# Five blocks of up columns per MLP instead of four: 2048 plain, then four times 512 plain and 1024 by Strassen's product

## The chip, the cores and the metric

The kernel runs on one core of a Trainium2 chip. The metric is the device time of one execution in microseconds; the median of three runs is given. The engines are called as in the profile: PE is TensorE, DVE is VectorE, ACT is ScalarE, POOL is GpSimd, and SP's queue issues most of the DMAs.

## The reference

A two-layer decoder trunk over 256 tokens of width 2048, all in float32. Layer 0 mixes by a state-space scan and by stick-breaking attention, layer 1 by a pooling mixer; each mixer is followed by the same MLP, and the MLPs are what the change is about. Cut to what matters:

```python
def sq_relu_mlp(h, w_up, w_down):        # h: (256, 2048)
    u = jax.nn.relu(h @ w_up)            # w_up: (2048, 8192)
    return (u * u) @ w_down              # w_down: (8192, 2048)

for layer in range(2):
    x = x + mixer(rms_norm(x, ...), ...)
    x = x + sq_relu_mlp(rms_norm(x, mlp_norm[layer]), mlp_w_up[layer], mlp_w_down[layer])
```

## The kernel before

**Precision.** Every float32 operand is split into two parts, `hi` (rounded to the type TensorE multiplies fast, by ACT, L235) and `lo` (what is left, by DVE, L236). A product is done as hi x hi + lo x hi + hi x lo, so each tile of weights costs three matmuls of a token half (128 tokens) by 512 columns.

**The stream of weights.** `plan()` writes down, by hand and before anything is issued, the order of all work as a list of units and of steps. A unit is a block of output columns, a step one load of up to 512 KB: two tiles of 128 x 512 or four of 128 x 256. `feed(i)` runs ahead of the products: SP's queue loads the raw weights of a step nine steps ahead into seven buffers (`raw`, L206), and `split(i)` splits them three steps ahead into four buffers each of `hi` and `lo`. A scheduler then orders the instructions of each engine by this order and by what is ready; each engine works through its own row in order.

**The MLP.** The 8192 hidden columns are done in four blocks of 2048. A block has two parts.

- Up: plain units of 256 columns (kind `up`). Their result stands with the hidden columns on the partitions, as the down product wants it. For each of the 16 tiles of a unit TensorE does two pairs of a 512-wide matmul (L963) and a 256-wide one (L965), 32 pairs a unit. At the end of a unit `finish` adds the halves (ACT L324, DVE L325), applies relu and the norm's row (DVE L874) and leaves the rest to `gen_u`: the square (ACT L681), its `hi` (ACT L279) and its `lo` (DVE L280). Two units fill one u tile of four rows.
- Down: four units of 512 output columns (kind `down`), each over the block's 16 rows of tiles of u, two rows and 12 matmuls (L971) a step, eight steps a unit. Each unit's result is added into `x_sb` by DVE (L834), one addition per token half.

The first block's up columns are all plain: eight units. In the other three blocks 1024 of the 2048 columns are plain, four units, and 1024 are done by Strassen's product of 2 x 2 blocks with seven products instead of eight (kinds `sa` and `sb`, matmuls L734). Both are issued during the down product of the block before: `sa` in 12 steps, `sb` in eight pairs of steps, whose weights DVE combines first by four subtractions a pair (L222 to L225). A step has two products of three 512-wide matmuls. `due(i)` says after how many of the 32 down steps the i-th piece comes. `gen_s` then puts the products together on DVE and ACT and turns the result by 16 transposes on TensorE (L294) during the next block's up units. It runs in `lane`, a queue of work that advances by one stage a step.

**The end of layer 0.** After the first column group of the last down product, `finish` loads what the pooling mixer wants into the buffers that u held: the bias into u's rows 0 to 3 and the scale into rows 4 to 7 (L850), the pooling matrix into rows 8 to 11 (L843). Each load waits until the last column group has read those rows. DVE multiplies bias and scale (L854) and adds them to `x_sb` (L765), ACT converts the matrix (L845). The normed `x_sb` is turned by transposes (L294), multiplied by `pool_w` (L971), its result scaled and split (ACT L863, DVE L864), and the pooling matrix applied (L776 to L780).

The lines that set the order:

```python
            for i in range(8 if b == 0 else 4):
                unit("w_up", D * layer, KT, b * FB + 256 * i, 256, "up", (layer, b, i), ...
            if b + 1 < NB:
                for kind in ("sa", "sb"): ...
    def due(i):
        return 1 + 10 * i // 12 if i < 12 else 13 + 19 * (i - 12) // 8
```

## Time and profile before

| what | value |
| --- | --- |
| three runs | 2163.53, 2164.75, 2165.72 us; median 2164.75 |
| the profiled execution, its own time | 2164.82 us |
| its span, first to last instruction | 2163.0 us |
| granted TensorE clock, mean | 1.000 |
| HBM read | 450.32 MB, mean of all DMA 210 GB/s |
| DMA engines busy in a block's down part (1170.4 to 1296.1 us) | 0.76, 251 GB/s |
| DMA engines busy in a block's plain up part (1124.2 to 1170.4 us) | 0.58, 182 GB/s |
| DVE busy in these two | 100.8 of 125.7 us; 29.1 of 46.2 us |
| ACT busy in these two | 69.6 of 125.7 us; 24.8 of 46.2 us |

Matmuls overlap in the profile: a busy time for a group of them counts the overlap twice, so the pace is read from start to start, or from the pieces of the chain of waits. An idle time before an instruction is given in brackets with what ended it. The rows that carry the argument stand in the prediction.

### The profile page before, as it was taken

What the parts mean: (1) busy time and instruction counts of PE and PEld (TensorE: products, weight loads), DVE (VectorE), ACT (ScalarE), POOL (GpSimd) and SP (SyncE); (2) the same over time, 40 slices, a digit from 0 to 9 for tenths busy, and PEclk for the clock granted to TensorE, in tenths of its full rate; (3) what the DMA queues carried; (4) which work ended last, traced back from release to release, by engine and by line L of the source; (5) the groups of instructions that cost most, each with busy time, mean ns of one, the idle gap of its engine ahead of it and who ended that gap; (6) DMA issues with size and microseconds to landing.
All of it is one profiled execution on the core that took longest, in us unless ns stands there. A gap on an engine that the chain in (4) does not pass through costs nothing.

```text
span 2163.0 us, 28389 instructions
## 1 busy us (share of the span) xinstructions
PE 2154.4 (100%) x10613; PEld 1820.6 (84%) x10613; DVE 1541.7 (71%) x1908; ACT 1203.2 (56%) x1401; POOL 21.7 (1%) x21
## 2 busy tenths in 40 slices
PE   9999999999999999999999999999999999999999
PEld 8888888888888888888888888878888888888888
DVE  6988766656545586876886886578778678678754
ACT  7665456665644465555555555456555555555543
POOL 0000000000000000000000000000000000000000
PEclk9999999999999999999999999999999999999999
DMA  9665455555665567777776776565677677677663
GB/s 334 204 204 166 159 184 166 175 166 166 207 192 191 170 197 240 245 232 215 248 247 202 246 253 186 187 224 162 197 257 250 194 245 243 214 247 238 224 204 117
DMA packets 129002, 454.32 MB, mean 210 GB/s; under 512 B 14496, under 2 KB 17248, under 8 KB 128608
## 3 DMA queue, kind: packets, MB, share of 16 engines
q1 hardware_dynamic: 128000, 451.36, 64.4%
q8 instruction: 83, 1.36, 0.3%
q10 hardware_dynamic: 864, 1.15, 0.2%
q14 instruction: 55, 0.45, 0.1%
HBM read 450.32 MB, written 2.13 MB: 209 GB/s over the span
## 4 chain that ended last, share of the span: by engine, by line
PE 97%; DVE 1%; DMA 1%; issue 0%; ACT 0%; SPq 0%; DVEq 0%; ACTq 0%
PE acc L971 58%; PE acc L963 16%; PE bg L734 10%; PE acc L965 9%; PE bg L294 1%; PE bg L522 1%; DVE lo L236 0%; DMA raw<-w_all 0%; PE bg L579 0%; PE bg L669 0%; PE bg L614 0%; DMA st<-prow_in 0%; DVE st L765 0%; PE bg L610 0%; PE bg L671 0%
## 5 line engine op out<-in xcount | busy, mean ns | idle before, releaser
L235 ACT ACTIVATE hi<-raw 128x1024 fp32r<-128x1024 f32 (+2 forms) x846 | 887.6, 1049 | 889.8 <-PE acc L971 586.2
L236 DVE TENSOR_TENSOR lo<-raw,hi 128x1024 fp32r<-128x1024 f32 (+2 forms) x846 | 1012.2, 1206 | 454.7 <-ACT hi L235 432.4
L971 PE MATMUL acc<-hi,st 128*128 128x512 f32 (+2 forms) x3840 | 1165.6, 386 | 0.9 <-ACT hi L235 0.9
L971 PEld LDWEIGHTS acc<-hi,st 128*128 128x128 f32 x3840 | 710.9, 188 | 142.1 <-ACT hi L235 2.4
L971 PE MATMUL acc<-lo,st 128*128 128x512 f32 (+2 forms) x1920 | 736.2, 385 | 0.4 <-DVE lo L236 0.3
L963 PE MATMUL acc<-st,hi 128*128 128x512 f32 x1568 | 552.4, 394 | 0.0
L965 PE MATMUL acc<-st,lo 128*128 128x256 f32 x1568 | 441.8, 282 | 0.0
L971 PEld LDWEIGHTS acc<-lo,st 128*128 128x128 f32 x1920 | 360.6, 188 | 74.1 <-DVE lo L236 2.2
L963 PEld LDWEIGHTS acc<-st,hi 128*128 128x128 f32 x1568 | 294.3, 188 | 62.1 <-issue 1.4
L965 PEld LDWEIGHTS acc<-st,lo 128*128 128x128 f32 x1568 | 296.3, 189 | 2.0 <-issue 1.4
L734 PE MATMUL bg<-hi,st 128*128 128x512 f32 x672 | 206.9, 389 | 0.0
L734 PEld LDWEIGHTS bg<-hi,st 128*128 128x128 f32 x672 | 126.1, 188 | 26.3
L734 PE MATMUL bg<-lo,st 128*128 128x512 f32 x336 | 130.7, 389 | 0.0
L734 PEld LDWEIGHTS bg<-lo,st 128*128 128x128 f32 x336 | 63.1, 188 | 13.0
L834 DVE TENSOR_TENSOR st<-st,acc 128x512 f32<-128x512 f32 (+1 forms) x74 | 46.4, 669 | 15.9 <-PE acc L971 15.6
L222 DVE TENSOR_TENSOR raw<-raw 128x512 f32<-128x512 f32 x48 | 33.1, 689 | 31.1 <-DMA raw<-w_all 31.0
L223 DVE TENSOR_TENSOR raw<-raw,raw 128x512 f32<-128x512 f32 x48 | 33.1, 690 | 20.7 <-DMA raw<-w_all 19.9
L282 ACT ACTIVATE st<-bg,prm 128x256 fp32r<-128x256 f32 x64 | 28.4, 467 | 22.5 <-DVE st L283 20.9
L325 DVE TENSOR_TENSOR ev<-acc,ev 128x512 f32<-128x512 f32 x40 | 27.4, 686 | 11.6 <-ACT ev L324 11.6
L283 DVE SCALAR_TENSOR_TENSOR st<-bg,prm,st 128x256 fp32r<-128x256 f32 x64 | 29.5, 481 | 8.2 <-ACT st L282 8.2
L225 DVE TENSOR_TENSOR raw<-raw 128x512 f32<-128x512 f32 x48 | 33.1, 690 | 1.0
L224 DVE TENSOR_TENSOR raw<-raw,raw 128x512 f32<-128x512 f32 x48 | 32.9, 686 | 0.2
(187 smaller groups left out, 949.7 us busy)
## 6 DMA issues: line engine op xcount, KB each, us to landing
raw<-w_all SPq DMA_DIRECT2D x818, 512.0 KB, 3.8
raw<-w_all SPq DMA_DIRECT2D x20, 256.0 KB, 2.8
st<-x_in SPq DMA_DIRECT2D x8, 512.0 KB, 7.8
st<-scr SPq DMA_DIRECT2D x8, 512.0 KB, 6.1
raw<-w_all SPq DMA_DIRECT2D x8, 288.0 KB, 8.1
st<-prow_in SPq DMA_DIRECT2D x2, 1024.0 KB, 6.3
st<-xt_in SPq DMA_DIRECT2D x6, 256.0 KB, 7.4
st<-pmat_in SPq DMA_DIRECT2D x1, 768.0 KB, 6.2
```

The source lines that it names most:

```text
L222: dve.tensor_tensor(raw[:, 0], raw[:, 1], raw[:, 0], ALU.subtract)
L223: dve.tensor_tensor(raw[:, 1], two[:, 0], raw[:, 1], ALU.subtract)
L224: dve.tensor_tensor(two[:, 0], two[:, 0], raw[:, 0], ALU.subtract)
L225: dve.tensor_tensor(two[:, 1], two[:, 0], two[:, 1], ALU.subtract)
L235: act.activation(hi, raw, AF.Copy)
L236: dve.tensor_tensor(lo, raw, hi.bitcast(F32), ALU.subtract)
L283: dve.scalar_tensor_tensor(dst[:, 1, c], ps, gain, dst[:, 0, c].bitcast(F32), ALU.mult, ALU.subtract)
L734: pe.matmul(sps[q], st[h], w[:, j], start=p == 0 and w is hi and h == 0, stop=p == KT // 2 - 1 and w is lo)
L834: dve.tensor_tensor(x_sb[m][:, cs], x_sb[m][:, cs], ps[:, m, : d["n"]], ALU.add)
L963: pe.matmul(ps[:, f].rearrange("p (h t) -> p h t", h=2), hi[:, kk, fs], t[:, :, c], start=first, stop=False)
L965: pe.matmul(ps[:, f, :T], lo[:, kk, fs], t[:, 0, c], start=False, stop=last)
L971: pe.matmul(ps[:, m, :n], t[:, h % 2, c, m * P : (m + 1) * P], (hi, hi, lo)[h][:, kk], start=first and h == 0, stop=last and h == 2)
```

## The change

The MLP of each layer is done in five blocks instead of four: one of 2048 plain columns, then four of 1536, of which 512 are plain (two units) and 1024 Strassen's. Of 8192 columns, 4096 are plain and 4096 Strassen's; before, 5120 and 3072. A later block's down product has 12 rows of tiles, so six steps a column group and 24 in all, and `due` spreads the Strassen steps over these 24. Work per weight element, the buffers and the lookahead are as before.

```diff
-FB = 2048
-NB = DFF // FB
+SW = 1024
+
+BLOCKS = ((2048, 0), (512, SW), (512, SW), (512, SW), (512, SW))
+NB = len(BLOCKS)
+BASE = [sum(map(sum, BLOCKS[:b])) for b in range(NB)]
...
-            for i in range(8 if b == 0 else 4):
-                unit("w_up", D * layer, KT, b * FB + 256 * i, 256, "up", (layer, b, i),
+            for i in range(BLOCKS[b][0] // 256):
+                unit("w_up", D * layer, KT, BASE[b] + 256 * i, 256, "up", (layer, b, i),
...
-            if b + 1 < NB:
+            if b + 1 < NB and BLOCKS[b + 1][1]:
                 for kind in ("sa", "sb"):
-                    unit("w_up", D * layer, KT, (b + 1) * FB + FB // 2, 512, kind,
+                    unit("w_up", D * layer, KT, BASE[b + 1] + BLOCKS[b + 1][0], 512, kind,
...
-                    unit("w_down", DFF * layer + b * FB, KT, c0, n, "down", (layer, b, c),
+                    unit("w_down", DFF * layer + BASE[b], sum(BLOCKS[b]) // P, c0, n, "down",
+                         (layer, b, c),
...
-    def due(i):
-        return 1 + 10 * i // 12 if i < 12 else 13 + 19 * (i - 12) // 8
+    def due(i, n):
+        a = 5 * n // 16
+        return 1 + a * i // 12 if i < 12 else a + 3 + (n - a - 3) * (i - 12) // 8
...
-            yield from to_ring(lambda m: (a, e)[m][:, q], u_blk[b % 2], 8 + 4 * q,
-                               slot(base + 2 + q), None)
+            yield from to_ring(lambda m: (a, e)[m][:, q], u_blk[b % 2],
+                               BLOCKS[b][0] // P + 4 * q, slot(base + BLOCKS[b][0] // 512 + q),
+                               None)
```

In the changed kernel the lines quoted here stand five lower up to L739 (L236 is L241, L279 is L284), six lower from L765 to L874 (L834 is L840, L854 is L860), and five lower again behind them (L963 is L968, L971 is L976).

What this moves shows at three places. The first is ACT's row at the last block of layer 0, where the last up unit ends. `ev` is that unit's result, `acc` the sum it comes from, `st` the u tile. Before, the unit is the fourth, and its u goes to the second half of the second tile:

```order
L235 ACTIVATE hi_1910_11097<-raw_1888_10950 128x1024
L324 ACTIVATE ev_1908_11091<-acc_68_11004 128x512
L235 ACTIVATE hi_1913_11116<-raw_1891_10972 128x1024
L681 ACTIVATE ev_1908_11091<-ev_1908_11091 128x512
L279 ACTIVATE st5_1901_11044<-ev_1908_11091 128x512
L235 ACTIVATE hi_1916_11137<-raw_1895_10998 128x1024
```

Now it is the second, and its u goes to the second half of the first tile:

```order
L240 ACTIVATE hi_1978_11283<-raw_1951_11110 128x1024
L329 ACTIVATE ev_1976_11277<-acc_70_11172 128x512
L240 ACTIVATE hi_1982_11309<-raw_1954_11132 128x1024
L686 ACTIVATE ev_1976_11277<-ev_1976_11277 128x512
L284 ACTIVATE st4_1980_11289<-ev_1976_11277 128x512
L240 ACTIVATE hi_1985_11327<-raw_1960_11166 128x1024
```

ACT's order is the same; the tile that L284 writes is now `st4`, which the down product reads in its second step and not, as `st5` before, in its fourth.

The second place is DVE's row in the stretch in which the `sb` steps are split, from the split that frees a buffer to the first subtraction on the weights that are loaded into it. Before, in the third block of layer 0, `raw_1714` is freed and `raw_1736` comes into its place:

```order
L236 TENSOR_TENSOR lo_1735_10064<-raw_1714_9962,hi_1734_10063 128x1024
L224 TENSOR_TENSOR raw_1726_10023<-raw_1726_10023,raw_1723_10005 128x512
L225 TENSOR_TENSOR raw_1726_10023<-raw_1726_10023 128x512
L236 TENSOR_TENSOR lo_1738_10082<-raw_1717_9974,hi_1737_10081 128x1024
L222 TENSOR_TENSOR raw_1736_10079<-raw_1736_10079 128x512
```

Now, in the second block, `raw_1464` is freed and `raw_1485` comes into its place:

```order
L241 TENSOR_TENSOR lo_1484_8592<-raw_1464_8488,hi_1483_8591 128x1024
L241 TENSOR_TENSOR lo_1487_8604<-raw_1467_8506,hi_1486_8603 128x1024
L228 TENSOR_TENSOR raw_1476_8554<-raw_1479_8573,raw_1476_8554 128x512
L229 TENSOR_TENSOR raw_1479_8573<-raw_1479_8573,raw_1476_8554 128x512
L241 TENSOR_TENSOR lo_1490_8622<-raw_1470_8518,hi_1489_8621 128x1024
L230 TENSOR_TENSOR raw_1479_8573<-raw_1479_8573 128x512
L227 TENSOR_TENSOR raw_1485_8601<-raw_1485_8601 128x512
```

Between the two stand two subtractions and a split before, three subtractions and two splits now. Over the eight pairs of a block such a distance was two subtractions and a split in half of them, or its like; now in one.

The third place is DVE's row at the end of layer 0, around the additions of the last column group (`acc_72` before, `acc_74` now) into the two halves of `x_sb` (`st12`, `st13`). Before, the bias's additions and two splits stand ahead of both:

```order
L765 TENSOR_TENSOR st12_849_4939<-st12_849_4939,st4_1936_11251 128x512
L765 TENSOR_TENSOR st13_850_4940<-st13_850_4940,st4_1936_11251 128x512
L236 TENSOR_TENSOR lo_2019_11738<-raw_1995_11602,hi_2018_11737 128x1024
L236 TENSOR_TENSOR lo_2022_11756<-raw_1999_11624,hi_2021_11755 128x1024
L834 TENSOR_TENSOR st12_849_4939<-st12_849_4939,acc_72_11608 128x512
L834 TENSOR_TENSOR st13_850_4940<-st13_850_4940,acc_72_11608 128x512
```

Now one of the two comes first, and the product with the scale and six bias additions (three such pairs) stand between them:

```order
L241 TENSOR_TENSOR lo_2067_11802<-raw_2043_11664,hi_2066_11801 128x1024
L840 TENSOR_TENSOR st12_849_4939<-st12_849_4939,acc_74_11690 128x512
L860 TENSOR_TENSOR st4_1999_11405<-st4_1999_11405,st5_2000_11406 128x512 x4
L771 TENSOR_TENSOR st12_849_4939<-st12_849_4939,st4_1999_11405 128x512
L771 TENSOR_TENSOR st13_850_4940<-st13_850_4940,st4_1999_11405 128x512
...
L840 TENSOR_TENSOR st13_850_4940<-st13_850_4940,acc_74_11690 128x512
```

The load that L860 (L854 before) waits for starts when the fourth step of the last column group is done; that group had eight steps and now has six.

More of the change, by code (lines that the diff above doesn't have):

```diff
@@ L117, in plan @@
                     at += 1
-                    while held and at >= due(20 - len(held)):
+                    while held and at >= due(20 - len(held), 2 * d["nk"]):
                         seq += held.pop(0)
@@ L945, in tile_trunk @@
                 b = d["arg"][1]
-                need(lambda: b == 0 or len(u_blk[(b - 1) % 2]) == 16)
-                for kk in range(KT):
-                    u_blk[b % 2].pop(kk, None)
+                need(lambda: b == 0 or len(u_blk[(b - 1) % 2]) == sum(BLOCKS[b - 1]) // P)
+                u_blk[b % 2].clear()
         ps = accs[u]
```

## The prediction

> **What bounds the kernel now.** I read the page's busy times and its chain of waits first.
>
> ```profile
> span 2163.0 us, 28389 instructions
> PE 2154.4 (100%) x10613; PEld 1820.6 (84%) x10613; DVE 1541.7 (71%) x1908; ACT 1203.2 (56%) x1401; POOL 21.7 (1%) x21
> ...
> PE 97%; DVE 1%; DMA 1%; issue 0%; ACT 0%; SPq 0%; DVEq 0%; ACTq 0%
> ```
>
> The chain that ended last lies 97% on TensorE, so a matmul taken away is worth its place in that chain, and a wait put before a matmul costs its full length. The profiled execution took 2164.82 us, 1.82 around a span of 2163.0; that is 0.07 from the median of 2164.75, so a sum made against 2164.82 holds for the median as well. The pieces of that chain in the third block of layer 0 give the prices:
>
> ```profile
> 1124.37 0.23 PE acc L963
> ...
> 1132.69 0.44 PE bg L294 x4
> ...
> 1170.52 2.73 PE acc L971 x12
> 1173.25 2.72 PE bg L734 x12
> 1175.97 2.72 PE acc L971 x12
> ```
>
> From 1124.37 to 1170.52 TensorE does the block's four plain up units and, between them, four groups of four transposes. 46.15 less 4 x 0.44 is 44.39 us for four units, which are 4 x 32 pairs of a 512-wide and a 256-wide matmul: 0.347 us a pair. Twelve Strassen matmuls (L734) take 2.72 us, as twelve of the down product do.
>
> **The change, by counts.** Per layer the plain up units go from 20 to 16 and one more pair of `sa` and `sb` comes. Removed: 44.39 us. Added: 56 products of three matmuls, 168 = 14 x 12, so 14 x 2.72 = 38.08 us, and the 16 transposes of one more `gen_s`, 1.76 us. That leaves 4.55 us a layer, 9.1 us for both. The down product keeps its number of matmuls; only the last column group, cut into two halves, changes:
>
> ```profile
> 2070.85 88.33 PE acc L971 x480
> ```
>
> Of these 480, three column groups are 24 steps of 2.72 us (65.3); the other 192 half-wide matmuls take 23.05, 0.120 each. Two halves cost 0.240 against 0.227 for one full matmul; the last block now has 12 rows of tiles instead of 16, so 24 such pairs become whole: 0.3 us. Counts alone: 2164.82 - 9.4 = 2155.4. Also added per layer are 12 loads of 512 KB with their splits, 32 subtractions and 8 additions into `x_sb` on VectorE. These lie beside TensorE; what they cost if that cover fails is in (c).
>
> **Waits that the change adds.** Four places, (a) to (d).
>
> (a) The first down product of the last block. The same sequence of ScalarE runs at the end of the last up unit in the kernel before, so its length can be read (a piece of the chain, then rows of the timeline: start, us, engine, line, what):
>
> ```profile
> 1342.41 2.73 PE acc L971 x12
> ...
> 1343.29 0.58 ACT L324 ACTIVATE ev<-acc 128x512 f32<-128x512 f32 x1
> 1344.94 1.07 ACT L235 ACTIVATE hi<-raw 128x1024 fp32r<-128x1024 f32 x1 [1.07 <-PE acc L971]
> 1346.01 0.63 ACT L681 ACTIVATE ev<-ev 128x512 f32<-128x512 f32 x1
> 1346.67 0.64 ACT L279 ACTIVATE st<-ev 128x512 fp32r<-128x512 f32 x1
> ...
> 1347.34 0.69 DVE L280 TENSOR_TENSOR st<-ev,st 128x512 fp32r<-128x512 f32 x1
> ```
>
> The last up matmul ends at 1342.41. The `hi` half of that unit's u is there 4.90 us later (1346.67 + 0.64), the `lo` half 5.62 us later. ScalarE stands in between for the split that waits until TensorE has left the first down step (1344.94), and the square is queued behind it. Before the change this unit is the fourth, its u is the operand of the fourth down step, three steps or 8.2 us on, and nobody waits. After it, the unit is the second, its u is the operand of the second step, 2.72 us on, and in the last block TensorE has nothing else in its row. It waits 4.90 - 2.72 = 2.2 us, does one matmul on the `hi` half (0.23) and waits 0.5 us for the `lo` half. 2.7 us a layer, 5.4 for both; between 4.4 (the `hi` half alone) and 6.4.
>
> (b) The second to fourth block have Strassen work to put there: in TensorE's order 12 matmuls of the first step and 14 of Strassen stand before the matmul in question, 26 x 0.227 = 5.9 us, and five more before the `lo` half is wanted, 7.0 us. The same chain in the third block before, with one more split in ScalarE's row:
>
> ```profile
> 1175.61 0.61 ACT L279 ACTIVATE st<-ev 128x512 fp32r<-128x512 f32 x1
> ...
> 1176.88 0.68 DVE L280 TENSOR_TENSOR st<-ev,st 128x512 fp32r<-128x512 f32 x1
> ```
>
> From 1170.52 these end after 5.7 and 7.04 us. The cover just holds: I take 0.1 us at each of six places, 0.5 in all, and 0 to 3 as bounds (half a microsecond each if one signal more lies between).
>
> (c) VectorE in the stretch where `sb` runs. Its pace there, from start to start in the timeline, and below that two rows of the table of waits (us in total, times, longest):
>
> ```profile
> 1209.60 1.22 DVE L236 TENSOR_TENSOR lo<-raw,hi 128x1024 fp32r<-128x1024 f32 x1
> ...
> 1213.91 1.07 ACT L235 ACTIVATE hi<-raw 128x1024 fp32r<-128x1024 f32 x1 [0.34 <-PE bg L734]
> ...
> 1266.31 0.69 DVE L224 TENSOR_TENSOR raw<-raw,raw 128x512 f32<-128x512 f32 x1
> 1266.92 1.22 DVE L236 TENSOR_TENSOR lo<-raw,hi 128x1024 fp32r<-128x1024 f32 x1
> 1268.05 0.68 DVE L225 TENSOR_TENSOR raw<-raw 128x512 f32<-128x512 f32 x1
> 1268.66 1.28 DVE L834 TENSOR_TENSOR st<-st,acc 128x512 f32<-128x512 f32 x2
> 1269.85 3.49 DVE L236 TENSOR_TENSOR lo<-raw,hi 128x1024 fp32r<-128x1024 f32 x3
> ...
> 1271.03 1.07 ACT L235 ACTIVATE hi<-raw 128x1024 fp32r<-128x1024 f32 x1 [1.65 <-PE acc L971]
> ...
> 1280.09 0.50 PE L971 MATMUL acc<-lo,st 128*128 128x512 f32 x1 [0.30 <-DVE lo L236]
> ...
> DVE raw L222 <- DMA raw<-w_all: 31.0, 23, 3.2
> DVE raw L223 <- DMA raw<-w_all: 19.9, 25, 2.8
> ```
>
> A split holds VectorE 1.13 us, a subtraction 0.61 to 0.72 (I take 0.64), an addition 0.60. Before, from the first subtraction of a block to its last `sb` split, VectorE has 33 splits, 32 subtractions and 5 additions, 60.8 us, and waits (31.0 + 19.9) / 6 = 8.5 us for weights: 69.3. TensorE's 17 down and 16 `sb` steps there are 17 x 2.72 + 16 x 1.36 = 68.0. So VectorE is already a little slower, and its reserve shows it. ScalarE refills a `hi` buffer when TensorE leaves it, four steps later; that start is the moment at which the step three splits earlier is taken up. The split that ends at 1210.82 is taken at 1213.91, 3.1 us in hand; the first of the three at 1269.85 ends at 1271.0 and is taken at 1271.03, nothing in hand; at 1280.09 TensorE waits 0.30 us. The stretch eats 3.1 us where the sum gives 1.3: 1.8 us are small gaps.
>
> After, the stretch has 31 splits, 32 subtractions, 7 additions: 59.7 us, for 15 down steps and 16 of `sb`, 62.6 us. That is 2.9 us in hand where there were 7.2, so all hangs on the waits for weights. A load starts when a split frees its buffer, and the waits of before fit a landing 3.6 us later (4.3 for the second buffer of a pair). Before, in half of the eight pairs only about 2.3 us of VectorE work stand between; after, in one pair, and 3.5 to 7 in the others. That gives some 3.2 us of waiting instead of 8.5: 59.7 + 3.2 + 1.8 = 64.7 against 62.6, and the loss of 2.1 is less than the 3.1 in hand. I take 1.0 us for all six new stretches; the bounds are 0 and, with the full 8.5, 6 x (59.7 + 8.5 + 1.8 - 62.6 - 3.1) = 26 us.
>
> (d) The end of layer 0. Here the chain of before already leaves TensorE (five pieces of the chain, then rows of the timeline):
>
> ```profile
> 1421.03 6.66 DMA st<-prow_in
> ...
> 1427.71 2.00 DVE st L854 x4
> ...
> 1433.83 2.27 DVE lo L236 x2
> 1436.10 0.61 DVE st L834
> ...
> 1436.75 0.44 PE bg L294 x2
> ...
> 1426.94 0.33 SPq L843 DMA_DIRECT2D st<-pmat_in  x1
> ...
> 1433.26 1.49 ACT L845 ACTIVATE st<-st 128x1536 fp32r<-128x1536 f32 x1
> ...
> 1443.06 0.75 DVE L864 SCALAR_TENSOR_TENSOR t<-acc,rstd,t 128x512 fp32r<-128x512 f32 x1
> ```
>
> The load of the scale goes into the buffer that held u's rows 4 to 7, so it starts when the fourth step of the last down group is done (1421.03) and is there 6.7 us later. Four products and six additions (L854, L765) follow to 1433.83, and behind them in VectorE's row stand two splits and the addition (L834) that the transposes at 1436.75 wait for, late by 0.32 us. The group now has six steps, not eight. From the end of its fourth step the path is 6.7 + 2.4 + 3.7 + 0.6 = 13.4 us (the two splits now stand ahead of it); TensorE has 0.44 + 2 x 2.72 to the end of the group and 2 x 2.72 + 0.3 of pool work before it wants the result: 11.6. It waits 1.8. The pooling matrix follows the sixth step, which is now the last: ScalarE converts it (L845) some 7.8 us after the group's end instead of 2.4, and the squares of the norm stand behind that. From the trace's durations in the new order (conversion, split, square and its read-out, 0.9 to the power's result as from 1439.54 to 1440.59, then on VectorE a split, four short evictions, two additions and L864), the first half of the pool's operand comes at 14.9 us after the group's end and the second, two splits later, at 17.8; TensorE arrives at 13.9 and 15.9. Two more waits of about 1.0 and 1.8. With 0.3 of before taken off: 4.3 us. Bounds 1.5 (the first wait alone) and 7 (each half as long again).
>
> **The sum:** 2164.82 - 9.4 + 5.4 + 0.5 + 1.0 + 4.3 = 2166.6 us, +0.1%.
>
> **A rule on the clock.** The longest time TensorE stood idle within the work of before is below a microsecond, and no slice shows a clock under full:
>
> ```profile
> 1467.59 0.51 PE L780 MATMUL bg<-t,st 128*128 128x512 f32 x1 [0.84 <-DVE t L864]
> ...
> PEclk9999999999999999999999999999999999999999
> ```
>
> The waits of (a) and (d) are two to three times as long. If each of the five dropped the clock to a half for one step of twelve matmuls, 2.72 us more each, the sum would be 2180. The Trainium skill, "TensorE: Matmul & The Clock Gate", section "Why this matters for your kernels", says that gaps of more than about 3 us between bursts of matmuls bring the half clock back. By that rule none of these waits, worked out as 2.7 at most, does so; no row here shows one of that length.
>
> **The rivals.**
> 1. *The cover holds everywhere.* The scheduler's order is made for such waits, and splits run 3 us ahead in most stages. Against it: in (a) nothing stands between, and in (d) the chain of before has no slack. If (a) and (d) cost half or less, 2155.4 + 2 to 5: about 2159, faster.
> 2. *VectorE becomes the bound in the Strassen stretch.* Place: the last splits of `sb` in the second to fourth block. For it: the reserve of before falls to nothing. Against it: fewer waits for weights in the new order. It decides from some 4.2 us of waiting per stretch on; each further microsecond costs TensorE six. At 6 us: 11 us in place of 1.0, 2177, slower.
> 3. *The clock drops in the new waits:* 2180.
> 4. *The change moves no work off TensorE.* By the counts above it has 168 matmuls fewer (256 - 168 - 16 = 72 a layer and 24 in the last column group); I leave this 0.02, at 2165.
>
> **How the numbers follow.** A measurement of this kernel can tell about 0.2%, 4.3 us, from no change: under 2160.4 is faster, over 2169.1 slower. The forecast, 2166.6 with a range of its own from 2161 to 2173 by the bounds of (a), (b) and (d), has 0.60: 0.47 within 0.2% and 0.13 above. Rival 1 has 0.12, rival 2 0.22, rival 3 0.04. Faster 0.12, same 0.49, slower 0.39. The range reaches from rival 1 to the middle of rival 2: 2159 to 2179.
>
> **What would show it.** In the profile after, TensorE's matmul count falls by 168 and its busy time by some 9 us; PE at the first down product of a layer's last block shows a wait on ScalarE (L284 after) of 2.2 us and on VectorE of 0.5; at the end of layer 0 its transposes wait some 1.8 us for the additions and the pool matrix product 1 and 2 us for its operand. The waits of the subtractions for weights should fall from 8.5 to about 3 us a stretch. TensorE waiting for `lo` inside the `sb` stretches, over 1 us a block, would make rival 2 right; a clock below full after a wait, rival 3; no wait at all at the two places of (a), rival 1.

## The result and the profile after

The changed kernel took 2178.72 us (median of five runs, 2176.48 to 2181.33) against 2165.72 before: a ratio of 1.0059, 95% interval 1.0048 to 1.0069. It is slower. The forecast was 2166.6 and the range 2159 to 2179, so the median lies just inside its upper end, near rivals 2 (2177) and 3 (2180); two of the five runs lie above 2179. The profiled execution took 2176.69, 11.87 more than the 2164.82 of before. From the page and the table of waits after (us in total, times, longest); the DMA row's last number is the median time from issue to landing:

```profile
span 2174.9 us, 28266 instructions
PE 2154.2 (99%) x10445; PEld 1807.9 (83%) x10445; DVE 1609.6 (74%) x2008; ACT 1226.4 (56%) x1419; POOL 21.7 (1%) x21
...
PE 90%; DVE 5%; DMA 3%; issue 2%; ACT 0%; SPq 0%; POOL 0%; DVEq 0%; ACTq 0%; POOLq 0%
...
raw<-w_all SPq DMA_DIRECT2D x844, 512.0 KB, 4.2
...
PE acc L976 <- DVE lo L241: 6.2, 6, 2.1
PE acc L976 <- ACT st L284: 4.4, 2, 2.2
PE bg L299 <- DVE st L840: 1.7, 1, 1.7
PE bg L786 <- DVE t L870: 0.9, 2, 0.7
PE bg L786 <- ACT t L869: 0.9, 2, 0.6
...
DVE raw L227 <- DMA raw<-w_all: 40.7, 32, 3.0
DVE raw L228 <- DMA raw<-w_all: 15.1, 21, 1.6
```

The matmuls went down by 168 as counted, and yet TensorE's busy time did not fall, where some 9 us less had been forecast. About 3 us of this is work at half the clock, at which a 512-wide matmul is busy 0.63 us in the profile instead of 0.39; the rest is put down to waits shorter than the modelled ends of matmuls, which no row shows one by one. Waits of TensorE that were 0.3 us for `lo` are now 6.2, and the chain that ended last lies 10% outside TensorE, mostly on VectorE and the weights' DMAs.

An idle time in brackets starts where the modelled end of the matmul before lies, so short waits hide in it. I therefore read the losses from lengths: a down part runs from the first down product of a block to the first up product of the next. In the chain of waits, for the second block of layer 0 after the change:

```profile
977.33 2.73 PE acc L976 x12
...
1081.40 0.23 PE acc L968
```

That is 104.07 us. The same two places were read for every block and every kernel below; the last part of layer 1, which no up product follows, ends with the start of its last matmul. 24 down steps and 28 Strassen steps are 456 matmuls of 0.2267 us, 103.37 us.

| kernel | six down parts with Strassen of blocks 2 to 4 | last down part, layer 0 | last down part, layer 1 | half-clock windows inside the work |
| --- | --- | --- | --- | --- |
| before (its six with Strassen: blocks 1 to 3, 32 steps each) | 751.94, by count 750.8 | 119.44 | 88.20 | 0 |
| after | 632.55 (104.07, 105.48, 104.21, 104.87, 106.12, 107.80) | 104.30 | 69.14 | 2 |
| 456 matmuls six times | 620.2 | | | |

The up parts came out as counted: 23.96 us for two units with their transposes, 46.15 before for four.

### The profile page after: what moved, and what is told of

Its sections match the earlier page's. It is cut to its first block, busy times and chain, and to the rows that moved or that the text cites. A ratio compares the mean times of both kernels' runs of the same rounds, so it can differ in the third digit from the quotient of the medians.

```text
span 2174.9 us, 28266 instructions
## 1 busy us (share of the span) xinstructions
PE 2154.2 (99%) x10445; PEld 1807.9 (83%) x10445; DVE 1609.6 (74%) x2008; ACT 1226.4 (56%) x1419; POOL 21.7 (1%) x21
## 4 chain that ended last, share of the span: by engine, by line
PE 90%; DVE 5%; DMA 3%; issue 2%; ACT 0%; SPq 0%; POOL 0%; DVEq 0%; ACTq 0%; POOLq 0%
PE acc L976 53%; PE acc L968 13%; PE bg L739 12%; PE acc L970 7%; DMA raw<-w_all 3%; DVE lo L241 3%; PE bg L299 1%; PE bg L527 1%; DVE st L840 0%; PE bg L584 0%; PE bg L674 0%; PE bg L619 0%; DVE raw L228 0%; DMA st<-scr 0%; DVE st L771 0%
## 5 line engine op out<-in xcount | busy, mean ns | idle before, releaser
L240 ACT ACTIVATE hi<-raw 128x1024 fp32r<-128x1024 f32 (+2 forms) x868 | 910.5, 1051 | 870.1 <-PE acc L976 545.2
L241 DVE TENSOR_TENSOR lo<-raw,hi 128x1024 fp32r<-128x1024 f32 (+2 forms) x868 | 1037.6, 1207 | 400.1 <-ACT hi L240 371.5
L976 PE MATMUL acc<-hi,st 128*128 128x512 f32 (+2 forms) x3824 | 1170.3, 388 | 5.4 <-ACT st L284 4.4
L976 PEld LDWEIGHTS acc<-hi,st 128*128 128x128 f32 x3824 | 710.0, 188 | 150.7 <-ACT st L284 7.0
L976 PE MATMUL acc<-lo,st 128*128 128x512 f32 (+2 forms) x1912 | 736.8, 387 | 6.4 <-DVE lo L241 6.2
L968 PE MATMUL acc<-st,hi 128*128 128x512 f32 x1312 | 464.8, 396 | 0.0
L976 PEld LDWEIGHTS acc<-lo,st 128*128 128x128 f32 x1912 | 360.0, 188 | 83.8 <-DVE lo L241 11.2
L970 PE MATMUL acc<-st,lo 128*128 128x256 f32 x1312 | 369.5, 282 | 0.0
L968 PEld LDWEIGHTS acc<-st,hi 128*128 128x128 f32 x1312 | 246.2, 188 | 51.8 <-issue 1.4
L739 PE MATMUL bg<-hi,st 128*128 128x512 f32 x896 | 277.0, 389 | 0.0
L970 PEld LDWEIGHTS acc<-st,lo 128*128 128x128 f32 x1312 | 248.0, 189 | 2.1 <-issue 1.4
L739 PEld LDWEIGHTS bg<-hi,st 128*128 128x128 f32 x896 | 168.2, 188 | 34.9
L739 PE MATMUL bg<-lo,st 128*128 128x512 f32 x448 | 174.5, 390 | 0.0
L739 PEld LDWEIGHTS bg<-lo,st 128*128 128x128 f32 x448 | 84.1, 188 | 17.8 <-DVE lo L241 0.5
L840 DVE TENSOR_TENSOR st<-st,acc 128x512 f32<-128x512 f32 (+1 forms) x90 | 57.2, 670 | 13.9 <-PE acc L976 13.6
L228 DVE TENSOR_TENSOR raw<-raw,raw 128x512 f32<-128x512 f32 x64 | 44.0, 687 | 15.3 <-DMA raw<-w_all 15.1
L229 DVE TENSOR_TENSOR raw<-raw,raw 128x512 f32<-128x512 f32 x64 | 43.9, 686 | 0.7
```

The costliest lines, as they stand in the source:

```text
L228: dve.tensor_tensor(raw[:, 1], two[:, 0], raw[:, 1], ALU.subtract)
L229: dve.tensor_tensor(two[:, 0], two[:, 0], raw[:, 0], ALU.subtract)
L240: act.activation(hi, raw, AF.Copy)
L241: dve.tensor_tensor(lo, raw, hi.bitcast(F32), ALU.subtract)
L739: pe.matmul(sps[q], st[h], w[:, j], start=p == 0 and w is hi and h == 0, stop=p == KT // 2 - 1 and w is lo)
L840: dve.tensor_tensor(x_sb[m][:, cs], x_sb[m][:, cs], ps[:, m, : d["n"]], ALU.add)
```

## The half clock

The mean granted clock of the profiled execution is 0.998, where it was 1.000 before. Windows of a quarter of a microsecond show where: at 1368.49 and at 2044.33 the granted clock falls from 1.00 to 0.50 and stays there for 3.41 us. The distance, 675.84, is 198 times 3.4133. In all later profiles the falls of one execution also lay on one grid of 3.413 us to within 0.01 us (1439.83, 2098.60 and 2166.87 in one: 193 and 20 periods). So I laid the windows on that grid. Columns: window, its length, busy time and instructions of PE, PEld, DVE, ACT, POOL, the granted clock, the DMA share, GB/s. Around the wait at the last block's first down product, in layer 0 and then in layer 1:

```profile
1365.08:1368.49 3.41, 1.13 (x4) 0.37 (x2) 3.24 (x5) 2.32 (x3) 0.00 (x0) 1.00 0.41 154
1368.49:1371.90 3.41, 3.25 (x8) 2.58 (x9) 0.10 (x1) 0.00 (x0) 0.00 (x0) 0.50 0.48 156
1371.90:1375.32 3.42, 3.42 (x17) 2.78 (x15) 1.23 (x1) 1.06 (x1) 0.00 (x0) 1.00 0.00 0
...
2102.36:2105.77 3.41, 2.44 (x11) 1.69 (x9) 2.58 (x4) 2.33 (x4) 0.00 (x0) 1.00 0.57 151
2105.77:2109.19 3.42, 1.93 (x7) 1.40 (x8) 1.85 (x2) 1.17 (x2) 0.00 (x0) 1.00 0.64 218
2109.19:2112.60 3.41, 3.41 (x16) 2.83 (x16) 1.16 (x1) 1.06 (x1) 0.00 (x0) 1.00 0.19 77
```

The two waits are equally long, 2.22 us. In layer 0 the wait lies in one window, TensorE is busy in it for 1.13 of 3.41 us, and the next window has half the clock. There a 512-wide matmul takes 0.427 us from start to start instead of 0.227, so that a window holds eight of them instead of fifteen: 1.6 us lost where it is full of work. In layer 1 a border cuts the wait in two, 2.44 and 1.93 us are left busy, and nothing follows. This is a hypothesis from one profile at this point; the experiments carry it on.

## The experiments

The kernels are all made from the changed one, except e8. The ratio is to the kernel before, run on the same chip beside it.

| run | what is different | median us (runs) | ratio, 95% interval | six down parts | last, layer 0 | last, layer 1 | half-clock windows |
| --- | --- | --- | --- | --- | --- | --- | --- |
| e1 | row order | 2169.31 (11) | 1.0013, 1.0004 to 1.0022 | 628.44 | 101.95 | 66.13 | 1 |
| e2 | pool buffers | 2173.01 (6) | 1.0033, 1.0021 to 1.0044 | 630.28 | 103.03 | 69.13 | 1 |
| e3 | subtractions later | 2167.50 (11) | 1.0008, 0.9999 to 1.0017 | 621.39 | 106.34 | 70.36 | 3 |
| e4 | `sa` in 5 steps | 2168.03 (11) | 1.0009, 1.0000 to 1.0018 | 621.13 | 104.72 | 70.73 | 2 |
| e5 | none (once more) | 2173.24 (5) | 1.0038, 1.0025 to 1.0052 | 629.44 | 104.21 | 69.14 | 1 |
| e6 | bias later | 2175.69 (5) | 1.0057, 1.0044 to 1.0071 | 629.25 | 104.16 | 70.31 | 2 |
| e7 | e1 + e3 + e6 | 2159.09 (9) | 0.9971, 0.9961 to 0.9980 | 620.26 | 104.18 | 66.11 | 2 |
| e8 | before, with e3 + e6 | 2164.21 (11) | 0.9994, 0.9985 to 1.0003 | | 119.03 | 88.20 | 0 |
| e9 | early loads | 2170.91 (6) | 1.0027, 1.0015 to 1.0038 | 629.66 | 100.53 | 69.17 | 1 |
| e10 | e1 + e3 + e9 | 2153.83 (5) | 0.9942, 0.9929 to 0.9956 | 620.27 | 96.00 | 66.12 | 0 |
| e11 | e10 without e1 | 2162.91 (11) | 0.9987, 0.9978 to 0.9995 | 621.34 | 99.03 | 70.70 | 1 |

The lengths and windows are of each kernel's profiled execution. A half-clock window makes the part in which it lies 1.2 to 1.6 us longer: layer 1's last part, with the waits of (a), is 69.13 to 69.17 us without one and 70.31 to 70.73 with one.

**e1, the wait of (a) taken away by the order of rows.**

```diff
-            for j, (k, e) in enumerate(zip(ks, ks[1:] + [d["nk"]])):
+            ends = dict(zip(ks, ks[1:] + [d["nk"]]))
+            if d["kind"] == "down" and d["arg"][1] and d["arg"][2] == 0:
+                ks = [0, 4, 6, 2] + ks[4:]
+            for j, k in enumerate(ks):
+                e = ends[k]
```

> The first down unit of every later block takes its rows in the order 0-1, 4-5, 6-7, 2-3, 8-11 (both operands follow, the sum is the same). Theory: the two waits of 2.2 and 0.2 us at the last block's first down products go (TensorE lost 2.8 us there each, by the lengths of the stretches), and the 1.4 us that the other six later blocks lost at the same place; with them goes the half clock that followed one of the two waits (1.75 us). Span 2174.9 - 5.6 - 1.4 - 1.7 = 2166 to 2168, median near 2170; the wait of 2.1 us for a lo part in the last Strassen stretch of layer 1 stays and so does a half clock behind it. Rival: rows 4 to 7 come from gen_s, and TensorE waits for those instead: the waits turn up one step earlier, on L287 or L288, and the time stays within 2 us of 2178.7.

Layer 1's last down part fell from 69.14 to 66.13, 3.0 us. The waits on L284 are gone and none on `gen_s` came in their place, so the rival falls. In layer 0 the wait of the transposes for the last column group's addition rose to 2.7 us, with a half clock behind it, and took about half of that layer's gain back: its part is 2.35 us shorter, where the wait of (a) and the half clock behind it had cost some 4.5. Median 9 us below the first measurement of the changed kernel, 4 below the second (e5); the theory's 2170 holds.

**e3 and e4, the Strassen stretch.** In e3 the first of a pair's four subtractions stays behind whatever stands before it in program order on VectorE:

```diff
-            dve.tensor_tensor(raw[:, 0], raw[:, 1], raw[:, 0], ALU.subtract)
+            tc.keep_in_program_order(dve.tensor_tensor(raw[:, 0], raw[:, 1], raw[:, 0], ALU.subtract))
```

> The first of a pair's four subtractions stays behind the split before it in VectorE's row, so that nine to ten us of VectorE's work stand between the split that frees a buffer and the first subtraction on its next load, instead of about 3.5. Theory: what costs TensorE 8.5 us in the six new Strassen stretches is a subtraction that waits in VectorE's row for its load (5.8 to 7.8 us a stretch, of which two waits of together 2 us always at the same place) with splits queued behind it that are already late. Then the waits of L227 and L228 for DMA fall below 2 us a stretch, the waits of 1.6, 0.3, 1.0, 0.3, 1.0 and 2.1 us for lo go to 0.3 or less, the half clock behind the last of them goes too: 2178.7 - 7 - 1.7 = 2170. Rival A (VectorE has more work than the stretch has time): same number and length of its instructions, so the lo waits stay, moved, 2178.7. Rival B (DMA is at its limit, loads land later): the waits for DMA stay near 6 us a stretch, only at other lines, 2178.7. Rival C: four subtractions in a row delay the hi part of ScalarE; waits on L240 appear and it is slower than 2180.

In e4 the order within VectorE's row is left to the scheduler and the stretch gets two down steps more:

```diff
-        a = 5 * n // 16
+        a = 10 if n == 32 else 5
```

> The twelve sa steps come within 5 of the 24 down steps instead of 7, so that the sb stretch has 17 down steps instead of 15, as before the change. VectorE gets 5.44 us more time and two more splits (2.3 us) in each stretch. Theory: the loss in the new stretches (1.5 us a block, 8.5 in all) falls to what the stretches of before lost (0.2 us a block): 2178.7 - 7 and less half clock, 2170 to 2172. Rival B (DMA at its limit): the bytes of a block are the same, waits only move to the sa stretch: within 2 us of 2178.7. Rival A (VectorE's work over the whole block): DVE is busy some 80% of the block, so the rival expects as little gain only if the denser sa stretch loses what the sb stretch wins.

Start, us, engine, line and what, of the timeline of VectorE and one row of TensorE's, at the place where the changed kernel loses most in the third block of layer 0:

```profile
1173.09 0.68 DVE L230 TENSOR_TENSOR raw<-raw 128x512 f32<-128x512 f32 x1
1175.13 0.69 DVE L227 TENSOR_TENSOR raw<-raw 128x512 f32<-128x512 f32 x1 [1.35 <-DMA raw<-w_all]
1176.47 0.69 DVE L228 TENSOR_TENSOR raw<-raw,raw 128x512 f32<-128x512 f32 x1 [0.65 <-DMA raw<-w_all]
1177.08 3.49 DVE L241 TENSOR_TENSOR lo<-raw,hi 128x1024 fp32r<-128x1024 f32 x3
...
1178.35 0.50 PE L976 MATMUL acc<-lo,st 128*128 128x512 f32 x1 [1.60 <-DVE lo L241]
```

VectorE stands 2.0 us at two subtractions whose weights have not landed. Of the three splits behind them the first needs nothing that is missing; it is only queued behind, and it is the one that TensorE waits 1.60 us for. The two subtractions belong to the sixth of the block's eight pairs, and at this place stand waits of 1.0 to 2.3 us together in all six new stretches (in one of them the second subtraction waits alone). In e3, over the same microseconds, the sixth pair begins only at 1179.86, without a wait; the four subtractions ahead of it are the fifth pair:

```profile
1172.31 1.23 DVE L241 TENSOR_TENSOR lo<-raw,hi 128x1024 fp32r<-128x1024 f32 x1 [0.17 <-ACT hi L240]
1173.45 0.68 DVE L227 TENSOR_TENSOR raw<-raw 128x512 f32<-128x512 f32 x1
1174.17 0.69 DVE L228 TENSOR_TENSOR raw<-raw,raw 128x512 f32<-128x512 f32 x1
1174.89 0.69 DVE L229 TENSOR_TENSOR raw<-raw,raw 128x512 f32<-128x512 f32 x1
1175.62 0.69 DVE L230 TENSOR_TENSOR raw<-raw 128x512 f32<-128x512 f32 x1
1176.23 3.71 DVE L241 TENSOR_TENSOR lo<-raw,hi 128x1024 fp32r<-128x1024 f32 x3
1179.86 0.68 DVE L227 TENSOR_TENSOR raw<-raw 128x512 f32<-128x512 f32 x1
```

In the whole of e3 no subtraction waits for a load, where it was 55.8 us before this edit, although the loads of the whole kernel land after the same 4.2 us in the median. The six parts come to 621.39. VectorE does as many instructions of the same length (a split 1208 ns in the mean, 1207 before this edit; a subtraction 683 to 693, 686 to 688), so rival A (too much work) falls; so does B (DMA at its limit). e4 reaches the same 621.13 with the waits for loads still there:

```profile
DVE raw L227 <- DMA raw<-w_all: 34.2, 28, 3.1
DVE raw L228 <- DMA raw<-w_all: 6.8, 10, 1.2
```

Of these 41.0 us, 24.3 lie in the six new stretches, 3.3 to 4.9 in each, and cost TensorE nothing there. The edit does two things at once: VectorE has 3.1 us more in hand per stretch, and the waits fall from 6.7 us a stretch to 4.1. Which of the two was enough e4 alone does not show.

The stretches that no edit touched show how waits and loss go together. In the changed kernel, from two windows of the table of waits, a part that loses little and the one that loses most:

```profile
DVE raw L227 <- DMA raw<-w_all: 4.7, 4, 1.9
DVE raw L228 <- DMA raw<-w_all: 1.0, 2, 0.7
...
DVE raw L227 <- DMA raw<-w_all: 5.2, 4, 2.5
DVE raw L228 <- DMA raw<-w_all: 2.6, 2, 1.6
```

The first two rows are of 977 to 1081 us, the last two of 1970 to 2077. Without such waits a part takes 103.56 us (e3, e11), or 103.38 with the row order of e1 (e7, e10). The six parts of the changed kernel have 5.8, 5.8, 6.3, 7.0, 7.3 and 7.8 us of these waits and lose 0.5, 0.7, 1.3, 1.9, 2.6 and 2.6 us against that, the last without its half clock. Over the 36 such parts of the six profiles in which neither the subtractions nor the spread of the steps was changed (after, e1, e2, e5, e6, e9), the loss is the waits less 5.0 us, to within 0.8. The parts with 32 down steps, in which VectorE has 4.3 us more in hand by the prediction's sums (7.2 against 2.9), lose nothing with waits of up to 8.7 us and 0.2 to 0.6 with 8.8 to 10.1. So in these runs the loss goes by the sum of the waits against the reserve, and e3 shows that the place of the subtractions in the row makes the waits.

Both medians lie 5 to 11 us below the changed kernel's two and within 0.2% of the kernel before. A miss: in e3 and e4 the wait for L840 grew to 2.8 and 2.5 us, and half clocks came behind it and behind the second wait of (a). Why it grew was not tried; with the loads of e9 it is gone.

**e2, e6 and e9, the end of layer 0.** Three ways to take the wait of (d) away. e2 uses the one buffer of u that the last block leaves free, e6 puts the bias's work behind the last column group's additions, e9 loads into buffers that Strassen's operands have left:

```diff
e2
-                    pl["mat"] = slot(7, (P, 12, P))
+                    pl["mat"] = slot(5, (P, 12, P))
-                    ... (slot(4 + i, (P, D), F32) for i in range(2))
+                    ... (slot(4 + 3 * i, (P, D), F32) for i in range(2))
e6
-                    for i in range(4):
-                        q = slice(512 * i, 512 * i + 512)
-                        dve.tensor_mul(pl["bias"][:, q], pl["bias"][:, q], pl["scale"][:, q])
...
-                lane.append(add_bias(cs))
+                if c == 3:
+                    lane.append(all_bias())
e9
-                    mat = slot(6, (P, 12 * P), F32)
+                    mat = slot(8, (P, 12 * P), F32)
-                    ... (slot(4 + i, (P, D), F32) for i in range(2))
+                    ... (slot(9 + 2 * i, (P, D), F32) for i in range(2))
```

`all_bias` does the four products, the first pinned in program order, and then the eight additions.

> The scale is loaded into the buffer that the last block leaves free (slot 7) and the converted pooling matrix goes to slot 5. Theory: the wait of 1.71 us of the transposes for L840 at the end of layer 0 goes, as the bias's additions now stand ahead of the last column group's; the four waits of the pool products (0.3 to 0.65 each, 1.8 together) stay, as the matrix still comes after the sixth step. Down part and pool of layer 0 shorter by 1.9 us, median 2176.8. Rival: the matrix's conversion is what ends last, and the pool's waits grow by what the transposes' wait loses: nothing gained, 2178.7.

> The product of bias and scale and the eight bias additions come behind the last column group's additions in VectorE's row. Theory: the wait of 1.7 us (after) to 2.8 us (in later runs) of the transposes for L840 falls to under 0.4, and a half clock behind it goes; of the pool's four waits (1.8 together) the first two may grow by up to 1 us, as the additions now stand among the pool's own work. Down part of layer 0's last block and pool: 104.3 + 3.6 becomes 102.5 + 4; span 1.5 to 3 below the changed kernel's. Rival: VectorE's 6 us of bias work only move into the pool stage and its operand (L870) is late by as much: nothing gained.

> The bias, the scale and the raw pooling matrix are loaded into buffers 9, 11 and 8, which Strassen's operands have left by then, so that nothing at the end of layer 0 waits for rows of u. Theory: the 1.7 us wait for L840 and the four pool waits (1.8 together) were the loads' starts alone; the last down part and the pool (104.2 + 3.6 us in the second run of the changed kernel, of which 2.8 are the first down product's wait and 1.7 the half clock) become 101.0 + 3.0 with that half clock, 99.3 + 3.0 without: 3 to 3.5 us less. Rival: VectorE's row is what is late there, with the evictions of the transposes and splits (as when the bias came last, where its 6 us only moved into the pool): then under 1 us is gained. Median 2170 against 2173 to 2179.

Against 104.21 in e5, each with one half clock in this part: e2 103.03, e6 104.16, e9 100.53. In e2 a wait of 0.69 us stays, as the bias still waits for u's rows 0 to 3; 1.2 of the 1.9 us are there. In e6 the wait for L840 is gone and a wait of 1.27 us in the pool has come: the rival was right, nothing is gained, and the median is no better. In e7 the moved work even makes a wait of 3.44 us. e9 takes 3.7 us away, the theory's 3 to 3.5 and a little more: the late start of the loads was the cause, and of the waits there only one of the pool's, 0.58 us, stays. Its median's distance from e5, 2.3 us, is less than that, since the half clocks differ from run to run.

**e5 and e11, the half clock; e7, e8 and e10, the sum.**

> The changed kernel once more, for a second profile. In the profiles so far the half clock came in windows of 3.41 us on a fixed grid, right behind a window in which TensorE was busy for 1.42 us or less (seven of seven), and never behind one in which it was busy for 1.70 us or more. Theory: that is the rule, and whether a wait of 2.2 us brings it depends on where the wait falls in the grid; so in this run each wait over 2 us is followed by a half clock exactly if its window of the grid has TensorE busy below 1.4 to 1.7 us, each such window costs 1.71 us, and the runs' times go with their mean clock. Rival: the clock falls at random or by the chip's state; then a wait with a busy share above 0.5 is followed by a half clock, or windows fall without a wait. Median 2176 to 2180 as before.

> Row order of e1, subtractions of e3 and bias of e6 together. Theory (the losses are independent and add): the six new stretches at 103.4 to 103.6 us, the last down parts at 101.5 or less and 66.1, no half clock inside the work: span 2153 to 2156, median 2156 (2155.4 was what the counts alone gave, plus about 1.4 us of pool waits), ratio to the kernel before 0.995 to 0.996. Rival (what one mends another takes): above 2160.

> The kernel before with the subtractions of e3 and the bias of e6, so that four and five blocks can be compared without waits in either. Theory: its down stretches fall from 125.1 to 125.7 to 125.1, 1.1 us in all, and the 0.3 us wait of the transposes goes; the pool's 1.5 us stay: median 2164.3, and the difference to e7 is 8 us, the 9.4 of the counts less the six places of 0.2 us before the lo half. Rival: the change of blocks itself is worth less than counted (under 5 us of difference).

> Row order, later subtractions and early loads together. Theory: six stretches at 103.4, last down parts 96.5 to 97.5 and 66.1, no wait over 1 us after the start, so no half clock in any run: clock 1.000, all runs within 2 us of each other, span 2151 to 2153, median 2154 (counts alone 2155.4 with the kernel before's own 1.8 us of pool waits and 1.1 us of Strassen waits in it, which go too). Ratio 0.9945 to 0.9955. Rival: the losses are not independent and another place waits instead: above 2158, with a wait over 1 us in the trace.

> The kernel of e10 with the rows in their old order, so that the waits of 2.2 us at the first down product of each layer's last block are the only ones over 1 us. Theory: each costs 2.8 us in every run (5.5 for both), the other six places 0.2 each, and a half clock of 1.71 us falls behind none, one or both, as the grid falls: 6.7 us over e10 with no half clock, 8.4 with one, 10.1 with two, and the runs' mean clock goes with it (1.000, 0.999, 0.998). Rival (half clocks come at random, or from DMA or VectorE): e10 shows them as well.

e5 is the changed kernel again; its median, 2173.24, lies below the 2176 to 2180 expected. Its five runs, 2172.56 to 2175.02, had mean clocks of 0.998 to 1.000; the first five, 2176.48 to 2181.33, had 0.996 to 0.998. A difference of 0.002 of 2175 us is 4.4 us, and most of the 5.5 between the medians is this. In e5's profile the two waits of 2.22 us leave 1.19 us busy in one window of the grid (a half clock follows) and 1.94 and 2.43 in two (none follows), as the theory has it. e11 has these two waits and, in the MLPs and the pool, no other over 0.6 us; windows on its grid:

```profile
1360.45:1363.87 3.42, 2.08 (x10) 1.39 (x8) 2.96 (x4) 2.35 (x4) 0.00 (x0) 1.00 0.57 172
1363.87:1367.28 3.41, 2.30 (x9) 1.68 (x10) 1.48 (x2) 0.80 (x2) 0.00 (x0) 1.00 0.68 225
...
2087.49:2090.91 3.42, 1.03 (x4) 0.29 (x2) 3.25 (x5) 2.32 (x3) 0.00 (x0) 1.00 0.51 153
2090.91:2094.32 3.41, 3.36 (x8) 2.68 (x9) 0.00 (x0) 0.00 (x0) 0.00 (x0) 0.50 0.50 154
```

Its parts are 3.03 us (layer 0) and 4.58 (layer 1, with the half clock) longer than e10's, and six times 0.18 comes from (b). By the lengths that makes 7.1 us over e10 with no half clock, 8.7 with one, 10.2 with two; its eleven runs lie 7.5 to 10.6 over e10's median. In e10 no half clock falls inside the work and the five runs lie within 1.1 us.

e7 missed its 2156 at the end of layer 0, by the pool's wait of 3.44 us and the half clocks behind it (a row of TensorE's timeline, then windows with two half clocks in a row); its three runs at a mean clock of 1.000 lie at 2156.3 to 2157.0:

```profile
1442.98 0.79 PE L795 MATMUL bg<-t,st 128*128 128x512 f32 x1 [3.44 <-DVE t L881]
...
1439.45:1442.86 3.41, 0.09 (x1) 0.00 (x0) 3.41 (x7) 0.51 (x1) 0.00 (x0) 1.00 0.00 0
1442.86:1446.27 3.41, 3.14 (x7) 1.99 (x8) 3.41 (x5) 0.69 (x1) 0.00 (x0) 0.50 0.33 100
1446.27:1449.69 3.42, 3.42 (x10) 2.65 (x9) 3.24 (x5) 0.00 (x0) 0.00 (x0) 0.50 0.56 212
```

e10, with the loads early instead, is the version that beats both kernels; its page and table of waits:

```profile
span 2152.6 us, 28255 instructions
PE 2144.0 (100%) x10445; PEld 1807.0 (84%) x10445; DVE 1624.9 (75%) x2008; ACT 1221.5 (57%) x1419; POOL 21.7 (1%) x21
...
PE 99%; DMA 0%; DVE 0%; SPq 0%; ACT 0%; issue 0%; DVEq 0%; ACTq 0%
...
PE acc L980 <- ACT hi L244: 1.6, 2, 1.3
PE bg L908 <- DVE ev L905: 1.5, 1, 1.5
PE bg L790 <- DVE t L874: 0.6, 1, 0.6
```

Of these waits only the last, 0.6 us, lies behind the first 13 us. VectorE is busy 15 us longer than in the changed kernel's page, with the same number of instructions, and TensorE 10 us less. e8, the kernel before with two of the mends, is at 2164.21 as expected, not clearly better than before; its difference to e7 is 5.1 us and not the 8 expected, by e7's miss. The difference to e10 is 10.4 us, of which 1.3 is the end of layer 0 (119.03 less eight steps, 97.27, against 96.00): five blocks are worth 9.1 us where nothing waits, and 9.4 had been counted.

## Why the prediction was right or wrong, point by point

The changed kernel's profiled execution, by the terms of the prediction's sum:

| term | predicted us | found us | from |
| --- | --- | --- | --- |
| counts | -9.4 | -9.3 | 8 x 23.96 - 6 x 46.15, 6 x 103.38 - 4 x 125.14, and eight steps less in each last part (21.8 and 22.1); e10 against e8, 9.1 |
| (a) last block's first down product | +5.4 | +6.0 | 99.03 - 96.00 and 69.14 - 66.12 |
| (b) the same in blocks 2 to 4 | +0.5 | +1.1 | (621.34 - 620.27) |
| (c) VectorE in the Strassen stretch | +1.0 | +8.7 | 632.55 - 1.6 - 621.34 = 9.6, + 0.2 and - 1.1 in 32-step parts |
| (d) end of layer 0 | +4.3 | +2.3 | 104.30 - 1.5 - 3.03 - 96.00 = 3.8, less 1.7 before (119.44 - 21.8 - 96.00), + 0.2 behind it |
| half clock | 0 | +3.1 | 1.6 in the full window at 2044.33; 1.5 at 1368.49, as e9's 100.53 against e11's 99.03 |
| sum | +1.8 | +11.9 | measured 11.87 |

**Counts: right.** They gave the gain to within 0.3 us, and e10 at 2153.83 shows that it is there to be had.

**(a): right**, with its place and its mechanism. The rows after read as those from which it was worked out; the split at L240 stands ahead of the square, and the two parts come at 1367.87 and 1368.59, 4.89 and 5.61 us after the last up matmul ends in the chain of waits (1362.98, the first row), where 4.90 and 5.62 had been worked out:

```profile
1362.98 2.51 PE acc L976 x11
...
1365.52 1.06 ACT L240 ACTIVATE hi<-raw 128x1024 fp32r<-128x1024 f32 x1 [1.07 <-PE acc L976]
1366.58 0.63 ACT L686 ACTIVATE ev<-ev 128x512 f32<-128x512 f32 x1
1367.24 0.63 ACT L284 ACTIVATE st<-ev 128x512 fp32r<-128x512 f32 x1
1367.90 0.69 DVE L285 TENSOR_TENSOR st<-ev,st 128x512 fp32r<-128x512 f32 x1
1367.92 0.50 PE L976 MATMUL acc<-hi,st 128*128 128x512 f32 x1 [2.22 <-ACT st L284]
```

**(b): right**, 0.2 us a place where 0.1 had been taken.

**(c): the step that failed.** The prediction named the stretch, the reserve of 3.1 us and its end, but took 1.0 us for what cost 8.7. The input that was wrong is the waits of the subtractions for weights, which were to fall from 8.5 to 3.2 us a stretch; they are 5.8 to 7.8 in the six new stretches, 6.7 in the mean. Behind it stands the landing time: the prediction took 3.6 us, fitted to the waits of before. The loads of such a stretch took 4.4 us in the median, in the kernel before (1209 to 1285 us, the first row) as after (1133 to 1200 us):

```profile
raw<-w_all SPq DMA_DIRECT2D x36, 512.0 KB, 4.4
...
raw<-w_all SPq DMA_DIRECT2D x31, 512.0 KB, 4.4
```

Each new stretch has six such waits; 0.8 us more at each would be 4.8 us, an estimate, and 3.5 us were missing. The prediction's rule, waits against reserve as a sum, with no loss up to 4.2 us of waits a stretch and one for one from there on, was nearer than its input: the parts show such a line with its start at 5.0. At 6.7 us of waits the rule gives 15 us for the six stretches, the line 10, and 9.6 were measured. Rival 2, VectorE as the bound in this stretch, is thus what came, by its own condition (more than 4.2 us of waiting) and by its sign, waits of TensorE for `lo` of over 1 us a block (6.2 us in six blocks); it had put 11 us. The two cures are e3, which takes the waits away by the place of the pair, and e4, which lowers them and gives VectorE time.

**(d): right in mechanism, half in size.** The wait for L840 was 1.7 us, predicted 1.8. The pool's own waits are four of 0.3 to 0.7 us, 1.8 together, where the prediction had 1.0 and 1.8; 1.5 us of such waits had been there before, and the sum did not take them off.

**The half clock: a term put at 0, and rival 3 in part.** In the first profile waits of 2.06 and 2.22 us brought a half clock, where each fell into one window; each cost 1.5 to 1.6 us and not the 2.72 of rival 3. The rule of the Trainium skill, "TensorE: Matmul & The Clock Gate", section "Why this matters for your kernels", names gaps of more than about 3 us. The two differ, and the measurement decides.

**Chances, and luck.** 0.49 stood on no change because (c) was set near its lower bound. The bounds were 0 and 26 us, and the nearest measured row, the kernel before's 8.5 us of waits per stretch, pointed to more. That 2178.72 lies inside the range is in part luck: (c) and the half clock came together, which no rival had, and (d) came out 2 us lower than forecast; how many half clocks an execution gets moved the median of the same kernel from 2178.72 to 2173.24.

## What to carry to other kernels

An engine that works through its row in order can be the bound at 74% busy: look for an instruction that waits for a load with late work queued behind it, and set its place in the row against the landing time measured in that stretch. The sum that counts is the engine's work and its waits: past its reserve, here 5.0 us of waits a stretch, each further microsecond went to TensorE. When a change takes reserve from a stage, mend the waits there with the change, or the gain that was counted turns into a loss; here each of three small edits gave back what it was found to cost, and together they turned +0.6% into -0.6%. A load that fills a buffer which late work still reads starts late; if an operand that is dead by then has left another buffer, load into that.

## What the runs showed of the hardware

In the profiles here the granted clock of TensorE changes only on a grid of 3.413 us that runs through the whole execution, and its place against the kernel's start differs from run to run. In ten profiles fourteen windows in which TensorE was busy for 0.09 to 1.42 of the 3.41 us were each followed by a window at half the clock; none followed a window in which it was busy for 1.68 us or more, eleven of them with 1.68 to 2.14. Two half-clock windows with 2.59 and 3.14 us busy were followed by a second one, and none of those with 3.19 or more. At half the clock a 512-wide matmul took 0.427 us from start to start instead of 0.227. So an idle time of about 2 us or more in one window can cost 1.2 to 1.6 us more, by chance of where it falls, and a kernel with several such waits spreads: the changed kernel's ten runs lie from 2172.6 to 2181.3, those of e10 within 1.1 us. The Trainium skill, "TensorE: Matmul & The Clock Gate", section "What's actually happening", has a free-running window of this length, and the runs agree; that a window need not be idle, only less than about half busy, is what they add. The window in which e1's matmuls end has 1.5 us busy, and a half clock follows it too; where between 1.5 and 1.68 us the border lies stays open.
